# Token mixer: rotations, relu and query splits in place in PSUM, low parts of weights on GpSimd, top-k block by block, first head among the projections

## The chip, the cores and the metric

The kernel runs on one core of a Trainium2 chip. The metric is the time of one execution on the device, in microseconds (us), smaller being better. The engines are TensorE (PE, its weight loads PEld), VectorE (DVE), ScalarE (ACT), GpSimd (POOL) and SyncE (SP, which issues most DMAs). Each runs its own instructions in a fixed order, and they wait for one another through semaphores.

## What is computed

One decoder layer for 512 tokens of 1024 features, in float32: a half-weighted SwiGLU feed-forward block, a token mixer, a second half-weighted SwiGLU block, and a final RMSNorm. Only the mixer differs between the two kernels:

```python
h = RMSNorm(x);  p = h @ W_in          # one projection, columns shared out
# group A: 8 heads of sparse attention; 16 indexer heads score every causal key
idx_logits = einsum('bqhd,bsd->bqhs', q_idx, k_idx)           # q_idx, k_idx, q, k rotated by position
score = einsum('bqh,bqhs->bqs', w_idx, relu(idx_logits))      # causal, else -inf
_, sel = top_k(score, 128)                                    # min(256, 512 / 4) keys for each query
p = softmax(where(selected, (q . k) * scale, -inf));  out_A = p @ v   # one k, v for the 8 heads
# group B: 8 heads of latent attention, dense causal
q = (rmsnorm(c_q) @ w_uq);  q_nope, q_pe = q[..., :64], rope(q[..., 64:])
kv = (rmsnorm(c_kv) @ w_ukv);  k_nope, v = kv[..., :64], kv[..., 64:]
p = softmax(((q_nope . k_nope) + (q_pe . k_pe)) * scale);  out_B = p @ v
x = x + concat(out_A, out_B) @ W_out
```

The indexer's scores decide which keys are selected, so they are computed as exactly as float32 allows: each operand is split into a high and a low part, and a product takes three matmuls.

## The kernel before

The work runs in three parts: first feed-forward block (to some 387 us of the profile), mixer (387 to 716 us), second feed-forward block. Matmuls work on tiles of 128 partitions by up to 512 columns. `split` (L93 to 95) makes a high part on ACT (`wh`) and a low part, the operand less its high part (`wl`), on DVE or POOL; `mm3` (L131 to 140) multiplies with both. All results of matmuls go through one group of eight PSUM banks (tile name `ps`).

In the mixer a string ORDER (L27) names steps, and for each the program writes the instructions; a scheduler then sets the order of each engine's instructions by its own model of their times. A set ON_VECTOR (L32) says which of the small operations go to DVE, the others going to POOL. The steps: `T`, `t`, `q0` to `q7`, `l0` to `l4`, `p`, `A0` to `A3`, `K`, `V` are projections from PSUM to SBUF; `s0` to `s7` ahead of the bar rotate the indexer's queries and lay out their parts in two tiles `qst` (`rope`, L615 to 629, `stack`, L637 to 647); `k`, `a` and `e` make the rotated keys (`kih`, `kil` for the indexer, `kah`, `kal` for group A, built by `doubled`, L663 to 671). `i0` to `i7` are the indexer's heads, two in each step (`index_heads`, L693 to 705): two matmuls into PSUM, relu on ACT into a tile `r` (four buffers), and one SCALAR_TENSOR_TENSOR on DVE that multiplies by the query's weight and adds to the scores `idx`, for the three blocks of 256, 384 and 512 keys. The first 128 queries need no selection.

`topk` (L708 to 718) finds the 128 largest scores of a query in 16 rounds. A round takes the eight largest of a row (MAX) and strikes them out (MATCH_REPLACE, with a MATCH_VALUE_LOAD ahead of it in the trace). A step `b` runs one round for each of the three blocks, MAX three times and then MATCH_REPLACE three times; the steps `b` stand among the others.

After the bar come the heads: `g` collects a head's operands (splits of queries `qf` and keys `kf`), `s` scores and softmax (L853 to 875: maximum on DVE by the instructions of L865, exponential and sum on ACT, L873), `z` normalises (L877 to 885: RECIPROCAL on DVE, products on POOL or DVE), `a` transposes the probabilities by PE (L950, L986), copies them to SBUF (L899 on DVE, L901 on ACT) and multiplies by the values (L953, L991). Units 0 to 7 are group B's heads; 8 to 15 are group A's, four heads of one query block each. `o` are the pieces of the output projection. In ORDER the scores of head n+2 or n+3 come before the probabilities of head n are used.

Of the kernel before, what the change touches and what calls it, by code (L numbers as in the profile page):

```python
# [184 lines left out]
def rows_of(k, col, out):  # L185
    nc = k.nc
    pb = k.tr()
    for t in range(NT):
        nc.tensor.matmul(pb[:, t * P:(t + 1) * P], col[:, t:t + 1].to_broadcast([P, P]), k.ident, start=True, stop=True)
    nc.scalar.activation(out, pb, AF.Copy)  # L190
    return out
# [196 lines left out]
def engine(nc, name):  # L388

    return nc.vector if name in ON_VECTOR else nc.gpsimd  # L390


def add_mixer_weights(k, w_in, w_uq, w_ukv, w_out):
# [9 lines left out]
    lo = lambda name: engine(nc, "w" + name)  # L403
# [27 lines left out]
    def rope_chunk(col, *names):  # L431
# [7 lines left out]
        def prep(j):  # L439
            def f():  # L440
                h, l = (w3(x, ND) for x in k.whl())
                for half in range(2):
                    src = c["r"][:, :, 128 * j:128 * j + 128].rearrange("p d (h s c) -> p d h s c", h=2, s=2)[:, :, :, half, :]
                    hv, lv = (x[:, :, 64 * half:64 * half + 64].rearrange("p d (h c) -> p d h c", h=2) for x in (h, l))
                    k.split(hv, lv, src, lo(names[j]))
# [773 lines left out]
```

## Time and profile before

| | |
|---|---|
| time, three runs | 1063.27, 1064.55, 1064.77 us, median 1064.55 |
| profiled execution | 1066.48 us, span of its trace 1064.7 us |
| busy | PE 1017.1, DVE 511.8, ACT 385.2, POOL 148.2 us |
| mixer, 387 to 716 us | PE 301.06, DVE 256.53, ACT 176.25, POOL 138.84 us of 329 |
| mean granted clock of TensorE | 0.985 |

Times in the rows are microseconds from the start of the span. "Busy" of PE counts matmuls whose ends are modelled, so a stretch in which it reads as full need not run at PE's best rate. A group's idle time is the time in which its engine stood still before the group's instructions, with the one that ended most of it.

### The profile page before, as it was taken

The page shows a single profiled execution, that of the slowest core. Times are in us where ns is not written, and L with a number is a line of the kernel's source. Part 1 is how long each engine was busy: PE and PEld are TensorE (multiplying, and loading weights), DVE is VectorE, ACT ScalarE, POOL GpSimd, SP SyncE. Part 2 cuts the span into 40 slices and gives each one's busy share as a digit, 9 for nine tenths or more (in the row PEclk, how much of TensorE's full clock was granted, in tenths as well). Part 3 has the DMA queues.
Part 4 walks back from the last instruction along what each step waited for, and adds up shares of the span by engine and source line. Part 5 has one row for each costly group of instructions (what it writes and reads, how often), then busy time and mean ns, then how long its engine had stood idle before and what let it go on. Part 6 is the DMA issues. An engine that isn't in the chain of part 4 may idle for free.

```text
span 1064.7 us, 12212 instructions
## 1 busy us (share of the span) xinstructions
PE 1017.1 (96%) x4726; PEld 832.1 (78%) x4726; DVE 511.8 (48%) x895; ACT 385.2 (36%) x691; POOL 148.2 (14%) x142
## 2 busy tenths in 40 slices
PE   5999999999999999889889999999999999999997
PEld 3888888888888888768765566888888888888886
DVE  5333332333333336989996768553333233333343
ACT  5322221122222335654367556353222212222222
POOL 1000000000000026533984222000000000000000
PEclk9999999999999999989988999999999999999999
DMA  8232233223323123322251001243323232222302
GB/s 289 77 109 79 79 119 119 79 79 100 108 90 97 40 79 98 119 76 100 85 162 54 6 1 60 83 154 119 119 79 118 81 103 95 79 80 99 118 1 80
DMA packets 83391, 98.84 MB, mean 93 GB/s; under 512 B 9027, under 2 KB 65475, under 8 KB 83333
## 3 DMA queue, kind: packets, MB, share of 16 engines
q1 hardware_dynamic: 83328, 98.06, 28.7%
q8 instruction: 37, 0.61, 0.2%
q14 instruction: 22, 0.17, 0.1%
q10 hardware_dynamic: 4, 0.00, 0.0%
HBM read 91.89 MB, written 2.10 MB: 88 GB/s over the span
## 4 chain that ended last, share of the span: by engine, by line
PE 80%; DVE 12%; ACT 3%; issue 3%; DMA 1%; POOL 1%; SPq 0%; POOLq 0%; DVEq 0%; ACTq 0%
PE ps L136 24%; PE ps L139 24%; PE ps L140 24%; DVE idx L713 2%; DVE s L712 2%; DVE idx L704 1%; PE ps L953 1%; DVE wl L95 1%; DMA raw<-in_w_up_dram 1%; PE ps L991 1%; DVE p L885 1%; PE ps L986 1%; PE ps L950 1%; DVE p L865 1%; PE ps L975 1%
## 5 line engine op out<-in xcount | busy, mean ns | idle before, releaser
L94 ACT ACTIVATE wh<-raw 128x1024 fp32r<-128x1024 f32 (+4 forms) x154 | 140.1, 925 | 386.5 <-PE ps L139 297.4
L95 DVE TENSOR_TENSOR wl<-raw,wh 128x1024 fp32r<-128x1024 f32 (+1 forms) x122 | 145.0, 1192 | 277.3 <-ACT wh L94 276.9
L136 PE MATMUL ps<-xh,wh 128*128 128x512 f32 (+2 forms) x712 | 267.0, 379 | 5.1 <-DVE res L1123 1.7
L139 PE MATMUL ps<-xh,wh 128*128 128x512 f32 (+2 forms) x712 | 268.0, 377 | 1.9 <-DVE xh L95 1.9
L140 PE MATMUL ps<-xh,wl 128*128 128x512 f32 (+2 forms) x712 | 267.9, 377 | 1.3 <-POOL wl L95 0.9
L136 PEld LDWEIGHTS ps<-xh,wh 128*128 128x128 f32 x712 | 134.4, 190 | 30.0 <-DVE f L622 2.1
L140 PEld LDWEIGHTS ps<-xh,wl 128*128 128x128 f32 x712 | 135.1, 190 | 25.2 <-POOL wl L95 1.3
L139 PEld LDWEIGHTS ps<-xh,wh 128*128 128x128 f32 x712 | 135.2, 190 | 25.0 <-DVE xh L95 2.2
L136 PE MATMUL ps<-wh,h 128*128 128x512 f32 x272 | 105.9, 389 | 0.0
L140 PE MATMUL ps<-wh,h 128*128 128x512 f32 x272 | 105.8, 389 | 0.0
L139 PE MATMUL ps<-wl,h 128*128 128x512 f32 x272 | 105.8, 389 | 0.0
L95 POOL TENSOR_TENSOR wl<-raw,wh 128x512 fp32r<-128x512 f32 (+5 forms) x32 | 43.3, 1374 | 403.7 <-ACT wh L94 399.1
L327 DVE TENSOR_TENSOR t<-ps,t 128x512 f32<-128x512 f32 x44 | 30.4, 692 | 141.3 <-PE ps L140 141.3
L94 ACT ACTIVATE w<-raw 128x1024 fp32r<-128x1024 f32 x32 | 34.0, 1061 | 118.3 <-PE ps L139 118.3
L136 PE MATMUL ps<-xh,w 128*128 128x512 f32 x176 | 68.5, 389 | 0.0
L140 PE MATMUL ps<-xh,w 128*128 128x512 f32 x176 | 68.5, 389 | 0.0
L139 PE MATMUL ps<-xh,w 128*128 128x512 f32 x176 | 68.5, 389 | 0.0
L283 POOL TENSOR_TENSOR fr<-tot,mhalf 128x1 f32<-128x1 f32 x12 | 7.3, 614 | 415.6 <-DVE tot L1166 360.1
L140 PEld LDWEIGHTS ps<-wh,h 128*128 128x128 f32 x272 | 51.0, 188 | 10.7
L136 PEld LDWEIGHTS ps<-wh,h 128*128 128x128 f32 x272 | 51.1, 188 | 10.6
L139 PEld LDWEIGHTS ps<-wl,h 128*128 128x128 f32 x272 | 51.1, 188 | 10.5
L95 DVE TENSOR_TENSOR w<-raw,w 128x1024 fp32r<-128x1024 f32 x32 | 39.2, 1225 | 29.6 <-ACT w L94 29.6
(214 smaller groups left out, 1349.5 us busy)
## 6 DMA issues: line engine op xcount, KB each, us to landing
raw<-in_w_up_dram SPq DMA_DIRECT2D x22, 1024.0 KB, 5.2
raw<-in_w_gate_dram SPq DMA_DIRECT2D x21, 1024.0 KB, 5.2
raw<-in_w_down_dram SPq DMA_DIRECT2D x20, 1024.0 KB, 5.0
raw<-in_w_in_dram SPq DMA_DIRECT2D x8, 1024.0 KB, 5.2
raw<-in_w_out_dram SPq DMA_DIRECT2D x4, 1024.0 KB, 5.3
res<-in_x_dram SPq DMA_DIRECT2D x4, 512.0 KB, 7.0
raw<-in_w_down_dram SPq DMA_DIRECT2D x4, 512.0 KB, 3.6
raw<-in_w_ukv_dram SPq DMA_DIRECT2D x2, 1024.0 KB, 4.9
```

The costliest lines, as they stand in the source:

```text
L94: self.nc.scalar.activation(hi, src, AF.Copy)
L95: (lo_engine or self.nc.vector).tensor_tensor(out=lo, in0=src, in1=hi.bitcast(F32), op=ALU.subtract)
L136: i = mm(out, wh, xh, start=first, stop=False)
L139: mm(out, wh, xl, start=False, stop=False)
L140: return i, mm(out, wl, xh, start=False, stop=last)
L327: nc.vector.tensor_tensor(out=u, in0=pu, in1=g, op=ALU.mult)
L704: nc.vector.scalar_tensor_tensor(out=score[i], in0=r, scalar=wt[:, i, h:h + 1], in1=cm(i) if h == 0 else score[i], op0=ALU.mult, op1=ALU.add)
L712: nc.vector.max(out=m8, in_=score[i])
L713: nc.vector.match_replace(out=score[i], in_to_replace=m8, in_values=score[i], imm_value=TAKEN)
L865: nc.vector.tensor_tensor_reduce(out=e, in0=p[:, :n], in1=bias, scale=1.0, scalar=-3.0e38, op0=ALU.add, op1=ALU.max, accum_out=mx[:, c:c + 1])
L885: nc.vector.tensor_scalar(out=e, in0=e, scalar1=rc[:, c:c + 1], scalar2=None, op0=ALU.mult)
L950: nc.tensor.transpose(p[:, i * P:(i + 1) * P], probs[i][:, j * P:(j + 1) * P], k.ident)
```

## The change

- `rope` works in place: the four operations read the projection in PSUM, the last two write back to it, and all four are on DVE. Before, the products by the sine of five rotations of 512 and three of 384 columns were made by POOL from a copy in SBUF that ACT made (L625 to 627), and ten of the additions (L628) were POOL's. The shared key of group B (`rotary_key`) is an exception: its rotation is now all POOL's, from SBUF.
- `stack` and the queries' splits read PSUM, on DVE; `qf` is no longer copied to SBUF. Splits of `kf` are all POOL's.
- `index_heads`: relu writes back into the PSUM bank, and DVE reads it there. The `r` tiles are gone.
- Low parts of the mixer's weights are all POOL's.
- `topk` takes one block after the other, and a step `b` is one pair of MAX and MATCH_REPLACE. Of the 48 pairs 33 stand before the bar, the other 15 in threes among the heads.
- Copies between halves of `kil` and `kal` leave DVE, for ACT and for two DMAs.
- The first head's `g0 s0` stands before the bar, ahead of `A3` and `V`; scores of head n+2 now come behind the use of head n (`s1 a0 s2 a1 s3 a2`).
- `normalise`: all products of heads 0 to 7 on POOL, all of units 8 to 15 on DVE. All copies of transposed probabilities are ACT's.
- A buffer of the probabilities lies in another pool, so that head 0 can begin earlier; memory for the heads' operands is taken when first needed.

The matmuls are the same in number and kind.

```diff
-        a, b = (f32()[:, n0:] for _ in range(2))
-        nc.vector.tensor_tensor(out=a, in0=p, in1=c, op=ALU.mult)
-        if "m" + name in ON_VECTOR:
-            nc.vector.tensor_tensor(out=b[lower], in0=p[upper], in1=s[upper], op=ALU.mult)
-            nc.vector.tensor_tensor(out=b[upper], in0=p[lower], in1=s[lower], op=ALU.mult)
-        else:
-            x = f32()[:, n0:]
-            nc.scalar.activation(x, p, AF.Copy)
-            nc.gpsimd.tensor_tensor(out=b[lower], in0=x[upper], in1=s[upper], op=ALU.mult)
-            nc.gpsimd.tensor_tensor(out=b[upper], in0=x[lower], in1=s[lower], op=ALU.mult)
-        engine(nc, name).tensor_tensor(out=a, in0=a, in1=b, op=ALU.add)
-        return a
+        b = f32()[:, n0:]
+        eng.tensor_tensor(out=b[lower], in0=p[upper], in1=s[upper], op=ALU.mult)
+        eng.tensor_tensor(out=b[upper], in0=p[lower], in1=s[lower], op=ALU.mult)
+        eng.tensor_tensor(out=p, in0=p, in1=c, op=ALU.mult)
+        eng.tensor_tensor(out=p, in0=p, in1=b, op=ALU.add)
+        return p
...
-                r = fr()[:, :n]
-                nc.scalar.activation(r, p, AF.Relu)
-                nc.vector.scalar_tensor_tensor(out=score[i], in0=r, scalar=wt[:, i, h:h + 1],
+                nc.scalar.activation(p, p, AF.Relu)
+                nc.vector.scalar_tensor_tensor(out=score[i], in0=p, scalar=wt[:, i, h:h + 1],
...
-        for _ in range(TOPK // 8):
-            for i in range(1, NT):
+        for i in range(1, NT):
+            for _ in range(TOPK // 8):
                 m8 = small(8)
                 nc.vector.max(out=m8, in_=score[i])
                 nc.vector.match_replace(out=score[i], in_to_replace=m8, in_values=score[i], imm_value=TAKEN)
-            yield
-        for i in range(1, NT):
+                yield
             nc.vector.tensor_scalar(out=score[i], in0=score[i], scalar1=TAKEN, scalar2=NEG, op0=ALU.not_equal, op1=ALU.mult)
...
-        qf[pr] = mp.tile([P, T], F32, tag="qf", name=k.name("qf"), bufs=1)
-        nc.scalar.activation(qf[pr], p, AF.Copy)
+        qf[pr] = p
...
-            if f"z{n}.{c}" not in ON_VECTOR:
+            if n < 8:
                 nc.gpsimd.tensor_tensor(out=e, in0=e, in1=rc[:, c:c + 1].to_broadcast(list(e.shape)), op=ALU.mult)
             else:
                 nc.vector.tensor_scalar(out=e, in0=e, scalar1=rc[:, c:c + 1], scalar2=None, op0=ALU.mult)
...
-            k.split(kh[r], kl[r], kf[pr][r], engine(nc, f"gk{h}"))
-            k.split(qh[r], ql[r], Mla.qf[r], engine(nc, f"gq{h}"))
+            k.split(kh[r], kl[r], kf[pr][r], nc.gpsimd)
+            k.split(qh[r], ql[r], Mla.qf[r])
...
-                taken(h, j, t[:, j * P:], p[:, j * P:])
+                nc.scalar.activation(t[:, j * P:], p[:, j * P:], AF.Copy)
...
-                    k.split(h[e], l[e], c["r"][:, 2 * j + e, :], lo("o7"))
+                    k.split(h[e], l[e], c["r"][:, 2 * j + e, :], lo)
```

On DVE, where the selection begins before, the three blocks take turns (`s` holds the eight maxima, `idx` a block's scores):

```order
L712 MAX s_3664<-idx_2657 128x8
L712 MAX s_3667<-idx_2658 128x8
L712 MAX s_3670<-idx_2659 128x8
L713 MATCH_REPLACE idx_2657<-s_3664,idx_2657 128x256
L713 MATCH_REPLACE idx_2658<-s_3667,idx_2658 128x384
L713 MATCH_REPLACE idx_2659<-s_3670,idx_2659 128x512
L712 MAX s_3673<-idx_2657 128x8
```

After, one block follows on itself, and each instruction needs the result of the one ahead of it:

```order
L692 MAX s_3597<-idx_2656 128x8
L693 MATCH_REPLACE idx_2656<-s_3597,idx_2656 128x256
L692 MAX s_3600<-idx_2656 128x8
L693 MATCH_REPLACE idx_2656<-s_3600,idx_2656 128x256
L692 MAX s_3603<-idx_2656 128x8
L693 MATCH_REPLACE idx_2656<-s_3603,idx_2656 128x256
L692 MAX s_3606<-idx_2656 128x8
L693 MATCH_REPLACE idx_2656<-s_3606,idx_2656 128x256
```

The three instructions of a kind stood together before; now one block's pair is repeated.

On DVE, where the selection ends after the change, its last rounds stand among the maxima (L838, which was L865) and the RECIPROCAL (L853, which was L880) of the first heads:

```order
L692 MAX s_4475<-idx_2658 128x8
L838 ISA p_4191,s_4188<-ps_4184,cmask 128x512
L838 ISA s_4188 128x1
L693 MATCH_REPLACE idx_2658<-s_4475,idx_2658 128x512
L844 TENSOR_TENSOR s_4190<-s_4188,scol_3816 128x4
L692 MAX s_4478<-idx_2658 128x8
L853 RECIPROCAL s_4201<-s_4101 128x4
L693 MATCH_REPLACE idx_2658<-s_4478,idx_2658 128x512
L692 MAX s_4481<-idx_2658 128x8
L693 MATCH_REPLACE idx_2658<-s_4481,idx_2658 128x512
L695 TENSOR_SCALAR idx_2658<-idx_2658 128x512
L838 ISA p_4272,s_4269<-ps_4254,cmask 128x128
```

Before, the selection's last instruction (L716) stands ahead of the first head's maxima:

```order
L716 TENSOR_SCALAR idx_2659<-idx_2659 128x512
L865 ISA p_4173,s_4170<-ps_4155,cmask 128x128
L865 ISA s_4170 128x1
L865 ISA p_4173,s_4170<-ps_4155,cmask 128x256
L865 ISA s_4170 128x1
L865 ISA p_4173,s_4170<-ps_4162,cmask 128x384
L865 ISA s_4170 128x1
```

Now the second head's RECIPROCAL stands behind the third head's maxima and between two rounds, and the fourth head's maxima directly behind the selection.

On PE, where the first head's probabilities are transposed (L950) and used (L953) before, scores (L935 to 937) of the fourth head follow:

```order
L950 MATMUL ps_4333<-ident,p_4173 128x128 x4
L953 MATMUL ps_4332<-h_4338,xh_4082 64x512
L950 MATMUL ps_4341<-ident,p_4173 128x128 x3
L950 MATMUL ps_4348<-ident,p_4173 128x128 x2
L950 MATMUL ps_4354<-ident,p_4173 128x128
L935 MATMUL ps_4359<-xh_4135,xh_4137 128x256
```

After the change (L923, L926 and L908 to 910 in their place), the third head's scores follow there, and the second head's probabilities (L923 on another tile) are wanted right behind them:

```order
L908 MATMUL ps_4184<-st_3895,st_3897 128x512
L909 MATMUL ps_4184<-st_3896,st_3897 128x512
L910 MATMUL ps_4184<-st_3895,st_3898 128x512
L926 MATMUL ps_4146<-h_4159,xh_4043 64x384
L926 MATMUL ps_4146<-h_4165,xh_4052 64x256
L926 MATMUL ps_4146<-h_4170,xh_4061 64x128
L923 MATMUL ps_4224<-ident,p_4103 128x128 x2
L923 MATMUL ps_4232<-ident,p_4103 128x128
L923 MATMUL ps_4224<-ident,p_4103 128x128
```

The scores ran three heads ahead of the probabilities' use before, and run two ahead now.

On POOL, among the first heads before, a part of the normalising products (L883) stands among the splits (L95); the others are DVE's:

```order
L883 TENSOR_TENSOR p_4173<-p_4173,s_4264 128x256
L95 TENSOR_TENSOR st_4132<-kf_3917,st_4131 64x512
L883 TENSOR_TENSOR p_4254<-p_4254,s_4298 128x128
L883 TENSOR_TENSOR p_4254<-p_4254,s_4298 128x256
L883 TENSOR_TENSOR p_4254<-p_4254,s_4298 128x384
L883 TENSOR_TENSOR p_4254<-p_4254,s_4298 128x512
L95 TENSOR_TENSOR st_4134<-qf_4322,st_4133 64x512
L95 TENSOR_TENSOR xh_4138<-qf_4322,xh_4137 64x512
L883 TENSOR_TENSOR p_4288<-p_4288,s_4425 128x128
L883 TENSOR_TENSOR p_4288<-p_4288,s_4425 128x256
L883 TENSOR_TENSOR p_4288<-p_4288,s_4425 128x384
L95 TENSOR_TENSOR st_4132<-kf_3919,st_4131 64x512
```

After, all four products (L856) of each of these heads are here:

```order
L856 TENSOR_TENSOR p_4103<-p_4103,s_4201 128x128
L856 TENSOR_TENSOR p_4103<-p_4103,s_4201 128x256
L856 TENSOR_TENSOR p_4103<-p_4103,s_4201 128x384
L856 TENSOR_TENSOR p_4103<-p_4103,s_4201 128x512
L90 TENSOR_TENSOR xh_4068<-kf_3829,xh_4067 64x512
L856 TENSOR_TENSOR p_4191<-p_4191,s_4309 128x128
L856 TENSOR_TENSOR p_4191<-p_4191,s_4309 128x256
L856 TENSOR_TENSOR p_4191<-p_4191,s_4309 128x384
L856 TENSOR_TENSOR p_4191<-p_4191,s_4309 128x512
L90 TENSOR_TENSOR st_3896<-kf_3831,st_3895 64x512
L856 TENSOR_TENSOR p_4272<-p_4272,s_4379 128x128
```

The four products of a head stand together now, and one split of `kf` stands ahead of each four.

## Rows read from the trace of the kernel before

**Rows 1.** The page's first part: busy time of each engine, its share of the span and its instructions.

```profile
PE 1017.1 (96%) x4726; PEld 832.1 (78%) x4726; DVE 511.8 (48%) x895; ACT 385.2 (36%) x691; POOL 148.2 (14%) x142
```

**Rows 2.** Busy time of each engine in stretches of the mixer (instructions in brackets: PE, PEld, DVE, ACT, POOL), then the granted clock of TensorE, the DMA engines' share and GB/s. The last row is the sum over the stretches from 387 to 716 us.

```profile
426.00:460.00 34.00, 29.31 (x151) 25.17 (x149) 33.64 (x43) 18.65 (x40) 17.48 (x11) 1.00 0.39 115
485.00:510.00 25.00, 25.00 (x127) 21.24 (x126) 25.00 (x73) 8.37 (x15) 13.29 (x13) 1.00 0.36 116
510.00:556.00 46.00, 38.46 (x171) 30.87 (x169) 45.94 (x103) 24.41 (x37) 42.72 (x34) 0.95 0.40 123
580.00:612.00 32.00, 30.03 (x154) 18.68 (x153) 24.19 (x76) 19.71 (x55) 9.37 (x9) 1.00 0.03 6
sum 329.00, PE 301.06 PEld 238.97 DVE 256.53 ACT 176.25 POOL 138.84; mean PE 27.37 PEld 21.72 DVE 23.32 ACT 16.02 POOL 12.62
```

**Rows 3.** What ended PE's waits from 370 to 715 us, the line with the most of it: total us, times, longest.

```profile
PE ps L700 <- DMA qst<-h: 4.1, 2, 3.0
```

**Rows 4.** Groups of instructions on DVE from 426 to 484.7 us, the stretch of the indexer's sums: line, operation, shapes, count | busy us, mean ns | idle before.

```profile
L704 DVE SCALAR_TENSOR_TENSOR idx<-r,wt,idx 128x512 f32<-128x512 f32 x15 | 14.8, 988 | 0.0
L704 DVE SCALAR_TENSOR_TENSOR idx<-r,wt,idx 128x384 f32<-128x384 f32 x15 | 12.0, 800 | 0.1
L704 DVE SCALAR_TENSOR_TENSOR idx<-r,wt,idx 128x256 f32<-128x256 f32 x15 | 10.0, 670 | 0.0
L95 DVE TENSOR_TENSOR wl<-raw,wh 128x1024 fp32r<-128x1024 f32 x2 | 3.3, 1632 | 0.8 <-ACT wh L94 0.8
L619 DVE TENSOR_TENSOR f<-ps,tab 128x384 f32<-128x384 f32 x5 | 2.8, 551 | 0.0
L735 DVE SCALAR_TENSOR_TENSOR lat<-ps,g_q_lat,lat 128x512 fp32r<-128x512 f32 x2 | 1.5, 748 | 3.3 <-ACT lat L734 3.3
```

**Rows 5.** The same sums on DVE alone in two stretches (same columns): ahead of the dots from 476.2 to 479.3 us, behind them from 479.3 to 484.6 us.

```profile
L704 DVE SCALAR_TENSOR_TENSOR idx<-r,wt,idx 128x384 f32<-128x384 f32 x1 | 1.6, 1640 | 0.0
L704 DVE SCALAR_TENSOR_TENSOR idx<-r,wt,idx 128x256 f32<-128x256 f32 x1 | 1.5, 1493 | 0.0
...
L704 DVE SCALAR_TENSOR_TENSOR idx<-r,wt,idx 128x512 f32<-128x512 f32 x4 | 3.0, 743 | 0.0
L704 DVE SCALAR_TENSOR_TENSOR idx<-r,wt,idx 128x384 f32<-128x384 f32 x3 | 1.8, 609 | 0.0
L704 DVE SCALAR_TENSOR_TENSOR idx<-r,wt,idx 128x256 f32<-128x256 f32 x3 | 1.4, 476 | 0.0
```

**Rows 6.** POOL's instructions from 475 to 484 us: start, us, line and operation, shapes [idle before].

```profile
475.04 2.41 POOL L95 TENSOR_TENSOR wl<-raw,wh 128x1024 fp32r<-128x1024 f32 x1 [8.60 <-ACT wh L94]
477.52 1.36 POOL L158 TENSOR_TENSOR f<-f,f 128x512 f32<-128x512 f32 x1
```

**Rows 7.** DVE's instructions in the order of time, where the keys' parts are finished and the sums begin, where the selection begins, where it ends, and at the first head's maxima: start, us, line and operation.

```profile
422.33 1.58 DVE L671 CAST kil<-kil 32x512 fp32r<-32x512 f32 x2
426.29 1.67 DVE L704 SCALAR_TENSOR_TENSOR idx<-r,wt,cmask 128x256 f32<-128x256 f32 x3
...
484.64 1.47 DVE L712 MAX8 s<-idx 128x8 f32<-128x256 f32 x3
...
554.43 1.48 DVE L716 TENSOR_SCALAR idx<-idx 128x512 f32<-128x512 f32 x1
555.83 0.28 DVE L865 CUSTOM_DVE_ANT_0 p<-ps,cmask 128x128 f32<-128x128 f32 x1
...
557.47 0.08 DVE L865 DVE_READ_ACCUMULATOR2_ANT s<- 128x1 f32 x1
557.58 0.16 DVE L871 TENSOR_TENSOR s<-s,scol 128x4 f32<-128x4 f32 x1
557.66 0.28 DVE L865 CUSTOM_DVE_ANT_0 p<-ps,cmask 128x128 f32<-128x128 f32 x1
```

**Rows 8.** Groups on DVE from 484.64 to 554.5 us, the selection (columns as in the fourth group of rows).

```profile
L712 DVE MAX8 s<-idx 128x8 f32<-128x512 f32 x16 | 10.8, 678 | 0.0
L713 DVE MATCH_REPLACE8 idx<-s,idx 128x512 f32<-128x512 f32 x16 | 10.8, 676 | 0.0
L712 DVE MAX8 s<-idx 128x8 f32<-128x384 f32 x16 | 8.7, 544 | 0.0
L712 DVE MAX8 s<-idx 128x8 f32<-128x256 f32 x16 | 6.7, 419 | 0.0
L619 DVE TENSOR_TENSOR f<-ps,tab 128x512 f32<-128x512 f32 x6 | 4.0, 672 | 0.0
```

**Rows 9.** The heads' products: a group on POOL from 370 to 715 us, and the four products of head 1 on POOL in the order of time; then the view of the line of DVE's products (count, ns min/median/max, first and last start) from 556 to 612 us.

```profile
L883 POOL TENSOR_TENSOR p<-p,s 128x512 f32<-128x512 f32 x6 | 6.9, 1164 | 3.7 <-DVE s L880 2.8 <-PE ps L991 0.9
564.91 2.76 POOL L883 TENSOR_TENSOR p<-p,s 128x128 f32<-128x128 f32 x4 [2.26 <-DVE s L880]
...
L885 DVE TENSOR_SCALAR p<-p,s x18: 275/476/2528, 561.6 to 603.5; 128x384 f32<-128x384 f32 x6, 128x512 f32<-128x512 f32 x5, 128x128 f32<-128x128 f32 x4, 128x256 f32<-128x256 f32 x3
```

**Rows 10.** PE's instructions in the order of time, from 566.1 to 576 us: six transposes, then scores of the fourth head; and the first and last of the scores of the fifth: start, us, line and operation, tiles.

```profile
566.18 1.54 PE L950 MATMUL ps<-ident,p 128*128 128x128 f32 x6
567.37 0.56 PE L935 MATMUL ps<-xh,xh 128*128 128x256 f32 x1
...
573.16 0.36 PE L935 MATMUL ps<-st,st 96*128 96x256 f32 x1
...
574.65 0.69 PE L937 MATMUL ps<-st,st 96*128 96x256 f32 x3
```

More of the change, by code (lines that the diff above doesn't have):

```diff
@@ L182, in rstd_of, with rows_of @@
     return col, m
-def rows_of(k, col, out):
+def rows_of(k, col, out=None):
     nc = k.nc
@@ L401, in w3 @@
         return x.rearrange("p (a b) -> p a b", a=a)
-    lo = lambda name: engine(nc, "w" + name)
+    lo = nc.gpsimd
     cell = {}
@@ L444, in f @@
                     hv, lv = (x[:, :, 64 * half:64 * half + 64].rearrange("p d (h c) -> p d h c", h=2) for x in (h, l))
-                    k.split(hv, lv, src, lo(names[j]))
+                    k.split(hv, lv, src, lo)
                 return h, l
@@ L468, in f @@
                 h, l = (w3(x, ND) for x in k.whl())
-                k.split(h, l, c["r"][:, :, j * P:(j + 1) * P], lo(names[j]))
+                k.split(h, l, c["r"][:, :, j * P:(j + 1) * P], lo)
                 return h, l
@@ L635, in quarters, with stack @@
         return [x[32 * q:32 * q + 32] for q in range(4)]
-    def stack(x, make, name, n0=0):
+    def stack(x, make, n0=0):
         out = [make()[:, n0:] for _ in range(2)]
         l = f32r()[:, n0:]
-        nc.scalar.activation(out[0], x, AF.Copy)
-        engine(nc, name).tensor_tensor(out=l, in0=x, in1=out[0].bitcast(F32), op=ALU.subtract)
+        k.split(out[0], l, x)
         nc.scalar.activation(out[1], x, AF.Copy)
@@ L1010, in out_part @@
             out_done(t, half, p, part == 0)
-    do = dict(g=lambda j: units[j].gather(), s=lambda j: units[j].score(), z=lambda j: normalise(j),
-              a=lambda j: units[j].apply(), o=out_part, n=lambda j: k.weights(ids[f"n{j}"]), b=background)
-    for w in steps[steps.index("|") + 1:]:
+    do = dict(T=keys, c=norm_column, t=rest, r=norm_rows, k=index_keys, v=rest_out, w=lambda j: values(v.x2),
+              e=lambda j: rotary_key(v.x2), q=index_queries, i=lambda j: index_heads(j, stacks.pop(j)), l=latent,
+              K=keys_b, R=keys_b_out, p=rotary_b, u=rotary_b_out, n=lambda j: k.weights(ids[f"n{j}"]), A=queries_a,
+              S=stack_a, V=values_b, b=background, x=index_stack,
+              g=lambda j: units[j].gather(), s=lambda j: units[j].score(), z=lambda j: normalise(j),
+              a=lambda j: units[j].apply(), o=out_part)
+    for w in steps:
+        if w == "|":
+            proj_scope.close()
+            attn.pool = mix.enter_context(k.tc.tile_pool(name="attn", bufs=1, reuse_waits="tile"))
+            continue
         do[w[0]](int(w[1:] or 0))
```

117 lines of the change are left out of this document (51 added, 66 removed).

## The prediction

> **What bounds the kernel now.** I read the page's first part first: PE is busy 96% of the span, DVE under half [rows 1]. That average hides the mixer, so I went to the table by stretches: of the mixer's 329 us PE is busy 301, so it stands still for 28; DVE is busy 256 of them, and in 426 to 460 us, 485 to 510 and 510 to 556 it has no gap left (33.6 of 34, 25 of 25, 45.9 of 46) [rows 2]. In those stretches PE's gaps are DVE's doing. The list of what ended PE's waits names many small ones, none over 4.1 us in sum [rows 3]; a chain like the indexer's (PE, ACT, DVE) spreads one late engine over all of them, so I reckon by stages, not by waits. Three stages matter: the indexer's sums, 426.3 to 484.6 us; the selection, 484.6 to 555.9; the heads behind it [rows 7]. The feed-forward parts are untouched and PE-bound.
>
> **The indexer's sums.** The 15 sums of each width took 988, 800 and 670 ns [rows 4]; in a quiet stretch the same sums took 743, 609 and 476 [rows 5]. The two slowest beside them (1640, 1493) ran under POOL's 2.41 and 1.36 us [rows 5, 6]: two SBUF operands on DVE beside a POOL operation that reads SBUF. The change gives DVE's sum one operand in PSUM. At the quiet durations 15 x (0.245 + 0.191 + 0.194) = 9.4 us go. The Trainium skill, "SBUF — State Buffer" § Who interferes with whom, has the rule: two SBUF inputs contend with GpSimd's reads, at most one does not. By that rule all of the slowing goes; the rows agree as far as they show one side only, since before has no sum from PSUM. A `lat` operation of the same kind with a PSUM operand took 748 beside 743 [rows 4, 5], so I price the sum from PSUM as a quiet one.
>
> Two low parts of 1024 columns, 3.3 us, leave DVE here [rows 4], and the shared key's rotation goes to POOL. Against this, all four operations of five rotations are now here at some 0.55 us (551 the one that is shown [rows 4]) and five splits. Following the order, DVE's work from first to last sum falls from 58.3 us to an estimate of 41 to 43: 48 sums at quiet durations less their overlap, 25; five rotations, 11; splits and `lat` operations, 4 to 6. But PE then becomes the limit: it has the projections and all index matmuls in the same stretch. I take 50, halfway, with 43 and 57 as ends. What DVE writes into PSUM, and relu from PSUM to PSUM, no row prices. The nearest, a product from PSUM to SBUF, took 551 for 384 columns; I take the same, and leave 0.1 us either way for each of the 20 rotation operations, 2 us both ways.
>
> The stage can also start earlier. Before, the key's low half is ready when the two copies end at 423.9 [rows 7]; after, no sum and no split of the key waits for POOL, the copies are ACT's, and the queries' `qst` no longer wait for POOL's addition. I follow the rows to a first sum at 418, 8 us earlier, ends 3 and 12. So the sums end at 418 + 50 = 468, against 484.6: **−16.6 us**, ends −4 and −22 (both ends of both would be rare).
>
> **The selection.** Before, it took 71.3 us [rows 7]. After, DVE has between first MAX and last TENSOR_SCALAR: 16 rounds of three pairs. An independent DVE instruction starts some 0.08 us ahead of the end of the one before (557.66 against 557.58 + 0.16), a dependent one 0.03 behind it (557.58 against 557.47 + 0.08) [rows 7]. So MAX costs 678, 544 and 419 less 0.08, MATCH_REPLACE (676 for 512 columns) as much and its load [rows 8]; I take 1.40 us a round for the one and 1.57 for the other, 16 x 2.97 = 47.5. Block by block, the pairs stand behind each other at some 57 places: 57 x 0.117 = 6.6 us. The Trainium skill, "VectorE: DVE Perf Modes" § The DRAIN you can't avoid, says that a semaphore between two operations costs nothing extra; by it these 6.6 us would be 0. The rows speak against it.
>
> Into the same stretch come four more parts. Rotations of A0 to A3 and of the two `pe` tiles are wholly DVE's, 6 x 4 operations at 672 ns [rows 8] less overlap, 15.6 (before about 6, the rest POOL's); splits of `qa`, `pe` and the heads' queries, 6; three heads' maxima, each 1.83 us (555.83 to 557.66 [rows 7]) with its sums, 5.5; `kf`, `lat` and the last operations, 8. Out go five low parts. The sum is 47.5 + 6.6 + 15.6 + 6 + 5.5 + 8 = 89 us: **+17.7**, ends +13 (the dependences cost nothing) and +23 (POOL slows the splits and products beside it, as it slowed the sums). So the selection ends at 468 + 89 = 557, against 555.9: what the first stage gains, the second takes back. The maxima of heads 0 to 2 are done by then, and that is the point of the change.
>
> **The heads.** Before, products of head 1 start at 564.9, 9.0 us behind the selection's end, and head 7's last at 603.5 [rows 7, 9]. After, head 1's RECIPROCAL stands five instructions ahead of the selection's end, some 2.5 us: products at 554.5, **−10.4** for the place of head 1 (it holds what the two stages above came to). The next six heads I price by the chain that the order shows with scores two ahead: transposes 1.2 (566.18 to 567.37), scores 2.2 (573.16 to 575.3) [rows 10], last maximum and sums and RECIPROCAL 1.0 (0.68 and two small ones), products on POOL 2.76 [rows 9]: 7.2 us a head, and with the copies off DVE nothing else limits it. Six heads take 43.2 against 38.6 before: **+4.6**. Ends: 6.0 a head (PE's own work with the copies, −3) and 8.3 (a `kf` split of POOL's or a low part in between and 1164 ns for the widest product [rows 9], +11).
>
> **Behind the heads.** The group A units keep their order on PE. Their products go from a mix to DVE alone, where one of these took 476 ns in the median [rows 9] against POOL's 1164 for the widest; ACT gets all copies, and there a late ACT would be next. PE has some idle time there (of its 28 us, 14.2 lie in the stretches of [rows 2], 4.7, 0, 7.5 and 2.0; the other 14 ahead, between and behind them). **−2.5**, ends −5 and +3. ACT's 26 more copies and DVE's lost ones lie under PE's work; where they don't, they are in the +3.
>
> **How the numbers follow.** −10.4 + 4.6 − 2.5 = −8.3 us against the profiled execution's own 1066.48, 1058.2; that execution lies 1.9 above the median of the runs, so the forecast for the median is **1056**. About 0.2%, 2 us, is what a measurement here can tell from no change.
>
> **Forecast, chance 0.44:** 1050 to 1062.4, own range. The stages cancel, the heads start earlier and run a little slower.
>
> **Rival 1, PE-bound (0.20):** DVE frees itself so far that PE sets the pace in the sums (43 us, −22), the dependences cost nothing (+13), heads at 6.0. Then head 1's products start at 484.6 − 22 + 84.3 − 2.5 = 544.4, 20.5 us earlier, and with −2.6 and −5 it is −28, all terms at their good ends; half of the way there from the forecast is −18: 1047. All 28 us of PE's idle time [rows 2] bound it at 1036. For it speaks that DVE is full in just the stretches where PE stands still; against it, that the DVE work of the selection does not shrink.
>
> **Rival 2, it cancels (0.14):** 1062.4 to 1066.7. The first stage gains 8 instead of 16, since index matmuls wait for `qst` and its DMAs as before (4.1 us [rows 3]).
>
> **Rival 3, slower (0.22):** head chain by POOL. Everything a head needs from POOL (split of `kf`, four products) is in one line with the weights' low parts, and the next head's scores wait for the transposes behind it. At 8.3 us a head and 94 for the selection, whose last rounds hold up the RECIPROCAL of heads 1 and 2, the sum is −8.3 + 6.6 + 5 = +3.3, 1068; with half of the sums' gain it is 1076. With that selection it decides from 8.1 us a head: six times 0.9 and the 5 use up the gain and 2 more. For it speaks POOL's 1.16 us for a product that takes DVE half [rows 9]; against, that POOL is only 9.4 us of 32 busy there before [rows 2]. Here too the "Rules for kernel authors" of "VectorE: DVE Perf Modes" (the Trainium skill) speak against the change: copy from PSUM to SBUF first where several operations follow. The row for a product from PSUM, 551 for 384 columns, gives it no price of its own.
>
> That the change does not do what it says is no case of its own: the order shows the moves.
>
> The range, 1041 to 1070, leaves out some 0.06 below and 0.12 above. Faster by over 0.2% (under 1062.4): the forecast 0.42 of its 0.44, rival 1: 0.62. Within: rival 2 and 0.02 of the forecast, 0.16. Slower: 0.22.
>
> **What would show it.** Right: sums from PSUM near 0.74, 0.61 and 0.48 us with no 1.5 us ones; last sum near 468; the selection 85 to 92 us long, MAX and MATCH_REPLACE of one block with gaps behind each; RECIPROCAL of head 1 ahead of the selection's end; products of heads 2 to 7 about 7 us apart on POOL. Wrong: rotation operations in PSUM over 0.65 us for 384 columns, PE waiting for a PSUM bank in 460 to 550 us, or ACT's copies as the releaser of PE behind 612 us.

## The result

The changed kernel takes 1075.62 us (median of four runs, 1074.61 to 1078.06) against 1063.91 before (1063.11 to 1064.77): ratio 1.0113, interval 1.0094 to 1.0133. It is slower by 12 us, where 1056 was forecast and the range ended at 1070.

The profile after has a span of 1076.3 us, 11.6 longer than before. Its table of stretches (columns as in [rows 2]):

```profile
426.00:460.00 34.00, 32.02 (x165) 28.67 (x166) 27.35 (x52) 19.97 (x43) 16.47 (x10) 1.00 0.41 117
510.00:556.00 46.00, 31.57 (x125) 23.98 (x124) 43.81 (x105) 22.75 (x43) 18.60 (x16) 0.82 0.38 112
556.00:580.00 24.00, 19.09 (x82) 11.96 (x81) 12.75 (x41) 14.02 (x37) 10.59 (x14) 0.93 0.08 17
580.00:612.00 32.00, 25.13 (x112) 14.99 (x111) 8.85 (x34) 17.50 (x47) 13.32 (x16) 0.93 0.02 5
```

Up to 460 us the change does what was hoped: PE is busy 32.0 of 34 us where it was 29.3. Then it turns: in 510 to 556 us PE falls from 38.5 to 31.6 of 46, in 580 to 612 from 30.0 to 25.1 of 32. In the last of these DVE is busy for only 8.9 us, where it was 24.2: PE no longer waits for want of DVE's time. What ended PE's waits from 370 to 730 us (total us, times, longest):

```profile
PE ps L923 <- POOL p L856: 16.9, 20, 5.9
PE ps L908 <- DMA xh<-pe: 6.3, 1, 6.3
PE ps L964 <- ACT h L961: 4.3, 6, 1.1
```

Before, no line had more than 4.1 us [rows 3]. Now the transposes (L923) wait 16.9 us for the heads' products on POOL, and the second head's scores once for 6.3 us for a small transfer.

The sums went as forecast. DVE's rows, in the order of time (first sums, last group of sums, first MAX and second, last instruction of the selection), then the sums by width (columns as in [rows 4]):

```profile
418.48 1.01 DVE L684 SCALAR_TENSOR_TENSOR idx<-ps,wt,cmask 128x256 f32<-128x256 f32 x2 [0.76 <-ACT ps L683]
...
463.01 6.39 DVE L684 SCALAR_TENSOR_TENSOR idx<-ps,wt,idx 128x256 f32<-128x256 f32 x12
469.31 0.42 DVE L692 MAX8 s<-idx 128x8 f32<-128x256 f32 x1
...
470.29 0.43 DVE L692 MAX8 s<-idx 128x8 f32<-128x256 f32 x1
...
561.95 0.85 DVE L695 TENSOR_SCALAR idx<-idx 128x512 f32<-128x512 f32 x1
```

```profile
L684 DVE SCALAR_TENSOR_TENSOR idx<-ps,wt,idx 128x512 f32<-128x512 f32 x15 | 11.1, 743 | 0.0
L684 DVE SCALAR_TENSOR_TENSOR idx<-ps,wt,idx 128x384 f32<-128x384 f32 x15 | 9.1, 609 | 0.0
L684 DVE SCALAR_TENSOR_TENSOR idx<-ps,wt,idx 128x256 f32<-128x256 f32 x15 | 7.2, 477 | 0.1
L612 DVE TENSOR_TENSOR ps<-ps,tab 128x384 f32<-128x384 f32 x8 | 4.5, 558 | 0.1
```

First sum at 418.5 (418 was forecast), last ended at 469.4 (468), 743, 609 and 477 ns for one, which is [rows 5] and not [rows 4]. The selection ended at 562.8, 93.5 us behind its first MAX (89). Writing to PSUM cost DVE little here: a rotation's product took 558 ns for 384 columns beside 551 [rows 4] with its result in SBUF.

Now the heads. POOL's line in the order of time; each `p<-p,s` row is the four products of a head, from head 0 on, and the rows between are the splits of `kf` (one low part of weights, 589.1 to 591.4, is left out at the dots):

```profile
546.59 2.75 POOL L856 TENSOR_TENSOR p<-p,s 128x128 f32<-128x128 f32 x4 [2.13 <-DVE s L853]
557.71 1.27 POOL L90 TENSOR_TENSOR st<-kf,st 64x512 fp32r<-64x512 f32 x1 [8.37 <-ACT st L89]
559.76 2.75 POOL L856 TENSOR_TENSOR p<-p,s 128x128 f32<-128x128 f32 x4 [0.78 <-DVE s L853]
567.57 1.29 POOL L90 TENSOR_TENSOR xh<-kf,xh 64x512 fp32r<-64x512 f32 x1 [5.05 <-ACT xh L89]
568.94 2.75 POOL L856 TENSOR_TENSOR p<-p,s 128x128 f32<-128x128 f32 x4
577.48 1.27 POOL L90 TENSOR_TENSOR st<-kf,st 64x512 fp32r<-64x512 f32 x1 [5.79 <-ACT st L89]
578.72 2.74 POOL L856 TENSOR_TENSOR p<-p,s 128x128 f32<-128x128 f32 x4
584.98 1.29 POOL L90 TENSOR_TENSOR xh<-kf,xh 64x512 fp32r<-64x512 f32 x1 [3.52 <-ACT xh L89]
586.35 2.75 POOL L856 TENSOR_TENSOR p<-p,s 128x128 f32<-128x128 f32 x4
...
595.17 2.75 POOL L856 TENSOR_TENSOR p<-p,s 128x128 f32<-128x128 f32 x4 [3.75 <-DVE s L853]
604.45 2.75 POOL L856 TENSOR_TENSOR p<-p,s 128x128 f32<-128x128 f32 x4 [6.53 <-DVE s L853]
614.32 2.75 POOL L856 TENSOR_TENSOR p<-p,s 128x128 f32<-128x128 f32 x4 [7.12 <-DVE s L853]
```

Head 1's products start at 559.8, 5.1 us earlier than before [rows 9] (10.4 was forecast). Head 7's start at 614.3: six heads in 54.6 us, **9.1 us a head**. Before it was 6.3 (head 7's first product started at 602.7 there). From the start of head 1's products to the end of head 7's it is 57.3 us (617.1 less 559.8) against 39.1 before (564.9 to some 604 [rows 9]): 18.2 lost. Behind that 1.5 is gained. −5.1 + 18.2 − 1.5 = 11.6, the whole difference of the spans.

What a head consists of is seen from head 3's products to head 4's. PE's rows, DVE's, and two of POOL's rows above:

```profile
581.52 0.66 PE L923 MATMUL ps<-ident,p 128*128 128x128 f32 x4 [0.45 <-POOL p L856]
581.93 0.36 PE L908 MATMUL ps<-xh,xh 128*128 128x256 f32 x1
583.72 0.40 PE L910 MATMUL ps<-xh,xh 128*128 128x512 f32 x1
...
584.15 0.69 DVE L838 CUSTOM_DVE_ANT_0 p<-ps,cmask 128x512 f32<-128x512 f32 x1
584.97 0.17 DVE L853 RECIPROCAL s<-s 128x4 f32<-128x4 f32 x1
```

Products 578.72 to 581.46; the last four transposes wait for the last product and end by 581.93; scores of head 5 until 584.1; its last maximum 584.15 to 584.84, and only then, at 584.97, head 4's RECIPROCAL, which stands behind that maximum in DVE's line. On POOL a split of `kf` for head 7 (584.98, 1.29 us), released by the same scores, stands ahead of the products, which start at 586.35. On this chain nothing lies beside anything else: 2.74 + 0.47 + 2.2 + 1.0 + 1.2 is 7.6 us. The next three take 8.8, 9.3 and 9.9. Their RECIPROCALs come later still: behind scores that stand behind transposes and copies of the head before, behind the split of a finished head's output that waits for ACT (603.53), and behind the maxima of the first unit of group A (until 613.9).

### The profile page after: what moved, and what is told of

Read it like the earlier page. It is cut to its first block, busy times and chain, and to the rows that moved or that the text cites. A ratio compares the mean times of both kernels' runs of the same rounds, so it can differ in the third digit from the quotient of the medians.

```text
span 1076.3 us, 12170 instructions
## 1 busy us (share of the span) xinstructions
PE 1022.6 (95%) x4726; PEld 835.9 (78%) x4726; DVE 479.9 (45%) x880; ACT 386.3 (36%) x706; POOL 131.8 (12%) x127
## 4 chain that ended last, share of the span: by engine, by line
PE 86%; ACT 5%; DVE 4%; POOL 2%; issue 1%; DMA 1%; SPq 0%; POOLq 0%; DVEq 0%; ACTq 0%
PE ps L131 26%; PE ps L134 26%; PE ps L135 26%; POOL p L856 2%; PE ps L926 1%; DVE p L838 1%; ACT p L846 1%; ACT wh L89 1%; PE ps L923 1%; PE ps L964 1%; PE ps L959 1%; PE ps L908 1%; PE ps L948 1%; DMA raw<-in_w_gate_dram 1%; PE ps L949 0%
## 5 line engine op out<-in xcount | busy, mean ns | idle before, releaser
L90 DVE TENSOR_TENSOR wl<-raw,wh 128x1024 fp32r<-128x1024 f32 (+1 forms) x102 | 122.8, 1204 | 273.1 <-ACT wh L89 272.7
L90 POOL TENSOR_TENSOR wl<-raw,wh 128x512 fp32r<-128x512 f32 (+5 forms) x52 | 75.2, 1468 | 467.3 <-ACT wh L89 458.7
```

The lines of the kernel that those rows point to most:

```text
L90: (lo_engine or self.nc.vector).tensor_tensor(out=lo, in0=src, in1=hi.bitcast(F32), op=ALU.subtract)
```

## The experiments

Twelve kernels. Ratios are to the kernel before on the same chip; the changed kernel's own is 1.0113. The kernel before took 1063.3 to 1064.4 us beside the different groups of runs, so a difference in us to the changed kernel, which was not run again, is uncertain by about 1 us.

**Products on DVE.** One line of `normalise`:

```diff
-            if n < 8:
+            if n < 0:
```

> The changed kernel with one line different: the products of heads 0 to 7 on DVE instead of POOL. Theory A (the heads' chain: transposes, scores two heads ahead, maxima, RECIPROCAL behind them, a kf split and four products in POOL's line): a head falls from 9.1 us to 6.5 to 7, since 2.75 us of products become 1.5 and the 1.3 us split no longer stands ahead of them; six heads save 13 to 15, the selection pays 2 to 3 back: 1062 to 1066 us. Rival B (the heads start late because DVE's selection and a late transfer hold them up, the products hardly matter): within 4 us of the changed kernel, 1072 to 1078. Rival C (DVE's products lengthen DVE's own line more than POOL's did): slower, over 1078.

1067.85 us, ratio 1.0046 (1.0029 to 1.0063): 7.8 us of the 12 come back, where theory A gave 10 to 14. PE still waits 11.7 us for products, now DVE's, and 7.1 for the transfer. Rivals B and C fall; A is right in sign and too large.

**Scores three heads ahead.** The heads' steps in ORDER:

```diff
-V n1 g1 s1 z0 b3 g2 a0 s2 z1 b3 g3 a1 s3 b3 g4 z2 a2 s4 b3 z3 g5 a3 s5 z4 g6 b3 a4 s6 z5 g7 a5 s7 z6 b3 a6 s8 z7 g8 g9 b3 a7 s9 o0 z8 b3
+V n1 g1 s1 z0 b3 g2 s2 z1 b3 a0 g3 s3 z2 b3 a1 g4 s4 z3 b3 a2 g5 s5 z4 b3 a3 g6 s6 z5 a4 g7 s7 z6 a5 s8 z7 a6 g8 g9 a7 s9 o0 z8
```

> The changed kernel with the order of the heads' steps different: scores three heads ahead of the use of the probabilities again (s1 s2 a0 s3 a1 s4 a2), products still on POOL. Theory A: the products and the RECIPROCAL lie beside the scores of the next head, a head takes 6 to 6.8 us, 1058 to 1064. Rival B (late start): no change, 1072 to 1078. Rival D (it is POOL's time itself, kf split and products in one line): as in the run with products on DVE or less, 1066 to 1072.

1057.7 us, ratio 0.9946 (0.9931 to 0.996): 18 us faster than the changed kernel and faster than before, with every product still on POOL. (The edit moves the selection's steps `b3` with the heads' and ends them one short: the selection's last TENSOR_SCALAR, L695 for 512 columns, is left out here and in the next run, so the last 128 queries are not masked as they should be. A later run has it again.) POOL's products from head 0 on:

```profile
547.54 2.76 POOL L856 TENSOR_TENSOR p<-p,s 128x128 f32<-128x128 f32 x4 [0.91 <-DVE s L853]
551.14 2.76 POOL L856 TENSOR_TENSOR p<-p,s 128x128 f32<-128x128 f32 x4 [0.85 <-DVE s L853]
563.08 2.76 POOL L856 TENSOR_TENSOR p<-p,s 128x128 f32<-128x128 f32 x4 [2.05 <-DVE s L853]
571.61 2.75 POOL L856 TENSOR_TENSOR p<-p,s 128x128 f32<-128x128 f32 x4 [0.19 <-DVE s L853]
574.74 2.76 POOL L856 TENSOR_TENSOR p<-p,s 128x128 f32<-128x128 f32 x4 [0.38 <-DVE s L853]
585.10 2.76 POOL L856 TENSOR_TENSOR p<-p,s 128x128 f32<-128x128 f32 x4 [2.58 <-DVE s L853]
588.11 2.75 POOL L856 TENSOR_TENSOR p<-p,s 128x128 f32<-128x128 f32 x4 [0.25 <-DVE s L853]
593.77 2.75 POOL L856 TENSOR_TENSOR p<-p,s 128x128 f32<-128x128 f32 x4 [2.90 <-DVE s L853]
```

From head 1 on six heads take 42.6 us instead of 54.6 (7.1 a head), the last five 30.7 (6.1 a head). The start of head 1 moves too: head 0's RECIPROCAL comes at 547.2 (546.3 in the changed kernel), but head 1's follows it after 3.7 us instead of 13.3, and head 1's products start at 551.1 instead of 559.8. The two together, 12.0 and 8.6, are the 20.0 us between the spans within 0.6. A head's products take what they took; they lie beside other heads' scores. Theory A holds (its time is missed by 0.3 us, its 6 to 6.8 us a head holds for the last five only), B and D fall.

**Both.** The two edits together.

> The changed kernel with both: products of heads 0 to 7 on DVE and scores three heads ahead. Theory A: little more than the better of the two, since both take the same wait away: 1056 to 1063. Rival B: 1070 to 1076. If the two gains add up (over 20 us, under 1055), they are two causes, not one.

1055.3 us, ratio 0.9925 (0.991 to 0.994): 2.4 us more than the order alone, where the products alone gave 7.8. The gains do not add up: for the most part it is one wait.

**Selection in rounds.** `topk` as before, in the changed kernel:

```diff
-        for i in range(1, NT):
-            for _ in range(TOPK // 8):
-                m8 = small(8)
-                nc.vector.max(out=m8, in_=score[i])
-                nc.vector.match_replace(out=score[i], in_to_replace=m8, in_values=score[i], imm_value=TAKEN)
+        for _ in range(TOPK // 8):
+            ms = []
+            for i in range(1, NT):
+                ms.append(small(8))
+                nc.vector.max(out=ms[-1], in_=score[i])
+            for i in range(1, NT):
+                nc.vector.match_replace(out=score[i], in_to_replace=ms[i - 1], in_values=score[i], imm_value=TAKEN)
                 yield
```

> The changed kernel with the selection in rounds over the three blocks as before (MAX three times, MATCH_REPLACE three times), all else the same. By the rows' gap of 0.117 us for each dependent neighbour (57 places, 6.6 us) the selection falls from 93.5 to 86 to 88 us and the heads start as much earlier: 1068 to 1071. If a dependent neighbour costs nothing extra: 1074 to 1077. If the heads' start doesn't hang on the selection's end (theory: chain of the heads alone): 1074 to 1077 as well, but with the selection shorter in the trace.

1077.25 us, ratio 1.0132 (1.0117 to 1.0147): nothing gained. The first two rounds' MAX in DVE's line:

```profile
466.75 1.48 DVE L693 MAX8 s<-idx 128x8 f32<-128x256 f32 x3
...
469.70 1.49 DVE L693 MAX8 s<-idx 128x8 f32<-128x256 f32 x3
```

A round of three pairs takes 2.95 us here. The selection took 80 us (466.7 to 546.8) instead of 93.5, but head 0's RECIPROCAL came at 546.3 as in the changed kernel, and head 1's products started at 559.1 beside 559.8. In the changed kernel these products start 3.0 us ahead of the selection's end, here 12.3 us behind it, with DVE idle for 8.6 us of that: head 1's start does not hang on that end. For head 0 the run does not separate two things, since in rounds its RECIPROCAL stands behind all of the selection but the last instruction. PE waited 7.1 us for the transfer here too.

**Relu in place alone**, in the kernel before:

```diff
-                r = fr()[:, :n]
-                nc.scalar.activation(r, p, AF.Relu)
-                nc.vector.scalar_tensor_tensor(out=score[i], in0=r, scalar=wt[:, i, h:h + 1],
+                nc.scalar.activation(p, p, AF.Relu)
+                nc.vector.scalar_tensor_tensor(out=score[i], in0=p, scalar=wt[:, i, h:h + 1],
```

> The kernel before with one part of the change: relu in place in PSUM and the indexer's sums reading PSUM, all else as before. Theory A (two SBUF operands on DVE beside POOL made the sums slow; from PSUM they take 743, 609, 477 ns): DVE loses 9 us of work in a stretch where it is full, the sums end 6 to 10 us earlier and with the selection full behind them the whole kernel gains as much: 1054 to 1058 us. Rival (the gain of the sums' stage in the changed kernel comes from the keys' earlier start and the low parts that left DVE): under 3 us, 1061 to 1064.

1057.8 us, ratio 0.9946 (0.9929 to 0.9963): 6.6 us faster. The widest sums in this kernel:

```profile
L703 DVE SCALAR_TENSOR_TENSOR idx<-ps,wt,idx 128x512 f32<-128x512 f32 x15 | 11.1, 740 | 0.0
```

POOL did what it did before, and the longest of the 45 sums took 0.75 us where it had been 2.87. The other widths took 606 and 474 ns, so the 45 sums need 9.6 us less of DVE, and the last one started 9.3 us earlier (474.7, before 484.0). The slowing in [rows 4] came from the second SBUF operand, and of the 9.3 us the whole kernel keeps 6.6.

**Products on POOL alone**, in the kernel before:

```diff
-            if f"z{n}.{c}" not in ON_VECTOR:
+            if n < 8 or f"z{n}.{c}" not in ON_VECTOR:
```

> The kernel before with one part of the change: all products of heads 0 to 7 on POOL, scores three heads ahead as before. Theory A (POOL's 2.75 us matter only where scores run two ahead): 0 to 3 us slower, 1063 to 1067. Rival D (POOL's products are late in any order): 8 or more slower, over 1071.

1062.81 us, ratio 0.9991 (0.9981 to 1.0): no loss. POOL's slower products cost nothing here, where scores run three ahead. Rival D falls.

**The second head's operands earlier**, in the changed kernel:

```diff
-A1 b6 K S0 A2 R b6 S1 b6 g0 s0 A3 b6 S2 S3 |
-V n1 g1 s1 ...
+A1 b6 K S0 A2 R b6 S1 b6 g0 s0 A3 b6 g1 S2 S3 |
+V n1 s1 ...
```

> The changed kernel with the second head's operands collected one step earlier (ahead of the bar), so that the transfers into the odd operands' tiles are issued ahead of the 1 MB weight transfer that they now stand behind; all else the same. PE's wait of 6.3 us for xh<-pe goes. If that wait sets the heads' start: 1068 to 1071. If DVE's selection, full up to 562 us, sets it as well: under 2 us gained, 1073 to 1077, and PE waits as long for the first products instead.

1072.35 us, ratio 1.0083 (1.0068 to 1.0098): 3.3 us faster, between the two cases (the intervals of this ratio and the changed kernel's overlap a little). PE's wait for the transfer is gone and head 0's RECIPROCAL comes at 540.9 instead of 546.3; the first transposes now wait 9.7 us for head 0's products.

**Both of these** (earlier operands and rounds):

> The changed kernel with both: operands of the second head collected earlier, and the selection in rounds over three blocks (each alone expected to be covered by the other: the run in rounds alone had the selection 13 us shorter and gained nothing). If the two waits cover each other, both taken away gain 5 to 8 us: 1067 to 1071. If neither sets the heads' start: 1073 to 1077.

1077.16 us, ratio 1.0126 (1.0105 to 1.0147): the 3.3 us are lost again. That the two waits cover each other is refuted; a third thing came in. In rounds, all of the selection stands ahead of the first RECIPROCAL in DVE's line: it came at 549.3 instead of 540.9, and PE stood still for 17.8 us in one piece up to head 0's first products. Only behind the RECIPROCAL had DVE 8.8 us free. How much of the selection stands ahead of that RECIPROCAL decides, not how long the selection is.

**The order of both, complete.** Scores three ahead and products on DVE, with the selection's last instruction (the difference to the run with both):

```diff
-... a3 g6 s6 z5 a4 g7 ...
+... a3 g6 s6 z5 b3 a4 g7 ...
```

> The changed kernel with products of heads 0 to 7 on DVE and scores three heads ahead, with the selection's steps among the heads complete (the two runs before this one with scores three ahead left out the last TENSOR_SCALAR of the selection, 0.85 us of DVE's work). Theory A: within 1.5 us of the run that left it out (1055.3), so 1054 to 1057, and faster than the kernel before. If that instruction was worth more than its length: over 1058.

1055.89 us, ratio 0.9924 (0.9909 to 0.9938). The missing instruction was worth its length at most.

**The same with the second head's operands earlier:**

> The same and the second head's operands collected earlier. The run with that alone gained 3.3 us; in the runs with scores three ahead PE still waited 7 us for the second head's scores. If that wait sets the heads' start here too: 1049 to 1053. If DVE's rounds ahead of the RECIPROCALs set it: 1053 to 1056.

**1051.2 us, ratio 0.9878 (0.9864 to 0.9893)**, faster than both kernels, by 12.6 and some 24 us. The edit gains 4.7 us here, and the first of the two cases came. What PE still waits for most from 400 to 730 us:

```profile
PE ps L923 <- DVE p L858: 5.4, 1, 5.4
PE ps L908 <- ACT st L89: 5.1, 3, 3.4
```

**The same with the selection in rounds:**

> The same and the selection in rounds over three blocks. In rounds the selection is some 10 us shorter, but all of it now stands ahead of the first RECIPROCAL on DVE. If what counts is how much of DVE's line stands ahead of the first RECIPROCALs: no better than the run block by block, 1052 to 1058. If what counts is the selection's end: 1045 to 1050.

1060.76 us, ratio 0.9968 (0.9957 to 0.9978): 9.6 us slower than block by block, and above the range of either case. Head 0's RECIPROCAL comes at 549.0 instead of 541.3. Here the block order of the change pays: it lets the RECIPROCALs stand between the rounds.

**Scores two ahead alone**, in the kernel before:

```diff
-g0 s0 n1 g1 b2 g2 b2 s1 z0 s2 z1 b2 g3 g4 a0 s3 a1 b2 g5 z2 s4 a2 b2 z4 g6 z3 s5 g7 a3 s6 g8 z5 b2 b2 g9 a4 s7 g10 a5
-b2 z6 s8 b2 a6 b2 b2 z7 a7 s9 o0 ...
+g0 s0 n1 g1 b2 b2 s1 z0 b2 b2 g2 a0 s2 z1 g3 a1 s3 g4 z2 a2 s4 z3 g5 a3 s5 z4 g6 a4 s6 z5 g7 a5 s7 z6 a6 s8 z7 g8 g9 g10 a7 s9 o0
...
```

> The kernel before with one thing changed: the heads' steps in the changed kernel's order, scores two heads ahead of the use of the probabilities; products as before, some on DVE and some on POOL. Theory A (the order is the cause): a head goes from 6.1 to 7 to 8 us, 6 to 13 us slower, 1070 to 1077. Rival D (the order costs only where all products are POOL's): under 3 us slower, 1063 to 1067.

1079.31 us, ratio 1.0144 (1.0129 to 1.0159): 15.5 us slower, above the top of what theory A gave. PE's waits for the heads' products:

```profile
PE ps L950 <- DVE p L885: 9.0, 3, 5.9
PE ps L950 <- POOL p L883: 5.2, 7, 2.3
```

From head 1's RECIPROCAL to head 7's it is 9.2 us a head (566.4 to 621.6), where the kernel before takes 6.3 (564.7 to 602.5): the changed kernel's 9.1, from the order alone. The order costs more than the whole change loses, and it costs it with a mix of DVE and POOL as well.

## Why the prediction was wrong

**The sums: right.** −16.6 us was forecast, −15.2 came (484.6 to 469.4). The 50 us for the stretch was halfway between two ends, so that it took 50.9 is in part luck. The price of a sum from PSUM held, and the run with relu in place alone shows the mechanism by itself. By the rule of the Trainium skill, "SBUF — State Buffer" § Who interferes with whom, an operation of the sums' kind with at most one SBUF input does not contend with GpSimd; the traces agree, 0.75 us for the longest sum beside 2.87.

**The selection: right in kind, 4.5 us short.** 93.5 us against 89. A dependent pair at 256 columns followed itself every 0.98 us (469.31 to 470.29), and the three pairs of a round in turns took 2.95 (466.75 to 469.70 in the run in rounds); that is 0.98 a pair for the mean of three widths against 0.98 for the smallest. So a neighbour that must wait did cost DVE time here. "VectorE: DVE Perf Modes" § The DRAIN you can't avoid in the Trainium skill, which the prediction set against this price, measures eight copies in a row, for which a semaphore costs nothing extra; these rows are another case. The run in rounds puts a size to it: of the 13.5 us by which its selection is shorter, some 3.0 are head 2's maxima and small operations that no longer fall into it, 2.7 are waits for ACT, and the 7.8 that are left are an estimate for the dependent neighbours, where 6.6 were priced. The 2.9 us of waits for ACT inside the changed kernel's selection had no term.

The step built on the selection, that the heads start by its end, was wrong, though head 1's products came 3.0 us ahead of that end and 2.5 were forecast: in the run in rounds they came 12.3 behind it, so that this agrees is chance. What the rows show in its place is a chain from head 0. Where scores run two ahead, head 1's products start 12.3 to 13.7 us behind head 0's RECIPROCAL (546.3 to 559.8 in the changed kernel, 546.3 to 559.1, 540.9 to 554.6 and 549.3 to 561.6 in the three runs with rounds or earlier operands), and 3.9 us behind it where they run three ahead (547.2 to 551.1). Head 0's RECIPROCAL in its turn comes at 540.9 where PE does not wait for the transfer, and at 549.3 where all of the selection stands ahead of it as well.

**The heads: the step that failed.** "7.2 us a head, and with the copies off DVE nothing else limits it" measured 9.1. The chain was the right one, and its own terms were nearly right (7.6 with the split in the shortest head). Missing were the split of `kf` ahead of the products in POOL's line (1.2 us, named in the upper end and not taken), transposes and copies ahead of the scores on PE, other DVE work ahead of the RECIPROCAL (up to 8 us of waiting for group A's scores), and head 7's own products at the end of the count (2.2 us). TensorE's clock is in it too: the scores ahead of head 2's products took 3.7 us (562.98 to 566.7, granted clock 0.54), those of the shortest head 2.2 at 1.00. Six heads: 54.6 for 43.2, 11.4 us, and the 2.2: that is 13.6 of the 19.9 us between the forecast's −8.3 and the measured +11.6 of the spans; the rest is head 1's start (5.3) and the stretch behind the heads (1.0).

The forecast took +4.6 as the cost of scores two ahead, six heads at 7.2 us, and nothing for head 1's start. The order alone, put into the kernel before, costs 15.5 us.

**Rival 3 named the right place and the wrong owner.** It blamed POOL's products and the splits in its line, and scores that wait for the transposes behind them, deciding from 8.1 us a head. 9.1 came. But all products on POOL cost nothing in the kernel before, and in the changed kernel the order gave back 18 us and the products 7.8. POOL's time is on the path only because the scores of a head wait for the use of the head two before. Its 1076 lies beside the measured 1075.6 by luck: it takes half of the sums' gain as lost, and nearly all of it came.

**Behind the heads:** −2.5 forecast, −1.5 came. **Rivals 1 and 2** need a head of 6.0 or 7.2 us and fall with the 9.1. Of the signs of being wrong that were named, none points at the step that failed: rotation operations took 558 ns, PE waits 0.3 us in 460 to 550 us for a bank that a sum still reads, and behind 612 us ACT's copies are indeed PE's main releaser, but with 4.3 us beside 4.1 for ACT's and DVE's copies before.

What stays open: how much of the time of head 0's RECIPROCAL DVE's line and the transfer each hold in the changed kernel. Earlier operands gained 3.3 us; the rounds, which shorten the selection, also move the RECIPROCAL behind it. Rotations and query splits in place were not tried alone.

## What to carry to other kernels

Price a pipeline's step as the full cycle: follow one item from a resource back to the same resource through every engine's line, with what is queued ahead in each line, and compare it with the bottleneck engine's own work; if the cycle is longer, try running one item further ahead before making instructions in it faster (18 us against 7.8 here). A RECIPROCAL of 0.17 us came 8.4 us later (549.3 for 540.9) for what stood ahead of it in DVE's line, so ask of each short instruction on the path what stands in front of it. A change can carry a good part (relu in place, 6.6 us) and a bad one (the order, 15 us): test them apart before the sum is believed.

## What the runs showed of the hardware

Small transfers that were issued behind a large one landed later here. SP's issues in the changed kernel, in the order of time, then the scores that waited, on PE:

```profile
525.51 2.44 SPq L617 DMA_DIRECT2D st<-pe  x4
528.07 0.50 SPq L62 DMA_DIRECT2D raw<-in_w_out_dram  x1
528.62 1.15 SPq L617 DMA_DIRECT2D xh<-kpe  x2
529.81 2.72 SPq L617 DMA_DIRECT2D xh<-pe  x4
...
535.07 1.30 PE L908 MATMUL ps<-xh,xh 128*128 128x256 f32 x3 [6.26 <-DMA xh<-pe]
```

The view of the DMA issues of that stretch (line, count, KB each, median us from issue to landing):

```profile
qa<-h SPq DMA_DIRECT2D x12, 64.0 KB, 2.0
st<-pe SPq DMA_DIRECT2D x4, 32.0 KB, 2.0
xh<-kpe SPq DMA_DIRECT2D x2, 64.0 KB, 5.5
xh<-pe SPq DMA_DIRECT2D x4, 32.0 KB, 3.8
```

Pieces issued at 525.5 landed 2.0 us after their issue; those issued at 528.6 and 529.8, behind 1 MB of weights from 528.07, took 5.5 and 3.8, and PE stood still for 6.3 us until they were there. Size alone does not explain it, since the pieces of `qa` with 64 KB took 2.0 as well. With the second head's operands earlier the transfers `xh<-pe` took 2.0 in the median. So the longer landing is 1.8 us for the last transfers that PE waited for, an estimate from 3.8 less 2.0; the rest of the 6.3 us lies in when they were issued.

TensorE's granted clock was 0.82 on average in 510 to 556 us, where PE stood still for 14.4 us. Two score matmuls of 512 columns, one after such waits and one later:

```profile
565.37 0.63 PE L908 MATMUL ps<-xh,xh 128*128 128x512 f32 x1
...
583.49 0.40 PE L909 MATMUL ps<-xh,xh 128*128 128x512 f32 x1
```

The granted clock of 563 to 566.4 us is 0.50, the level of 1.2 GHz, that of 582 to 584 us 1.00, 2.4 GHz. Ahead of the first, from 558.4 to 562.6 us, PE had stood still in four pieces of 0.2 to 1.8 us, 2.9 us together. Here the idle PE was paid for once more when its work came back: the scores of one head took 3.7 us in place of 2.2.
